# Mixture-of-experts kernel on one core: the row gather for a later expert moved inside the branch on a pair's second expert, and the row transposes for a missing second expert put under a branch

## The chip, the cores and the metric

One Trainium2 chip, one of its cores. The metric is the device time of one execution of the whole program in microseconds (us), lower being better. Engines: TensorE (PE; its weight loads appear as PEld), VectorE (DVE), ScalarE (ACT), GpSimd (POOL) and SyncE (SP, which here issues most DMA transfers). A name that ends in q, as in POOLq or PEldq, is an engine's instruction sequencer: branches, register loads and semaphore instructions run there.

## The reference

The program is two stacks of layers over 256 latent tokens of 1024 elements; layer 0 of the first stack also carries 256 context tokens. Two layers of attention with a mixture of experts come first, then two layers of another mixer with a dense feed-forward part. The change is inside the mixture of experts, of which this is the core (512 tokens in layer 0, 256 in layer 1):

```python
e_in = jnp.take_along_axis(e_logits, g_idx[:, :, None], 1)[:, 0]
top_v, top_i = lax.top_k(e_in, TOP_K_IN_GROUP)          # 2 of the 8 experts of the chosen group
experts = g_idx * EXPERTS_PER_GROUP + top_i             # 32 experts in all
...
def expert_block(a):
    xb, e = a
    return (jax.nn.silu(xb @ w1[e]) * (xb @ w3[e])) @ w2[e]
...
return jnp.zeros((t, d), h.dtype).at[tok_s].add(w_s[:, None].astype(h.dtype) * yb[dest])
```

Each token goes through two experts; an expert that no token chose needs no work. The weights are 1024x512 (w1, w3) and 512x1024 (w2) in float32, 6 MB per expert.

## The kernel before, in words

The routing part of a layer puts the experts into an order of "slots" and leaves the number of rows of each slot in a small table (`meta2`; `meta` for slots 0 and 1). The number of used slots depends on the data, so the part that runs the experts is control flow: every engine loads the counts into registers (`load`, recorded at line L1096, an instruction TENSOR_LOAD) and branches.

Slots 0 and 1 run first (L1197 to L1199, before the change). The rest runs in pairs: `pair(k)` takes the even slot k and then the odd slot k+1, the latter only where its count is positive (L1188), and at its end (L1193, L1194) calls itself inside a branch for slot k+2, where that has rows. The program text therefore holds all pairs one inside the other, and the branch at L1194 that isn't taken leaves the whole of it.

A slot's work, `turn`, reads the slot's rows, already transposed, from a buffer `XT` (there are two, by the parity of the slot), multiplies by the expert's weights, which SP fetches in six pieces of 1 MB (`expert_weights`, issued at L143), and ends with a `scatter` on POOL (L1002), an indirect DMA that puts the result rows into the DRAM buffer `ybuf`. A turn has variants by the number of rows: `quarter1` and `quarter2` up to 32 rows (PE lines L1020, L1029, L1037), `half1` and `half2` up to 64 (L1048, L1056, L1063), `full1` and `full2` for 128 (L1073, L1081, L1088).

Rows come two slots ahead. `ahead(k)` makes POOL issue an indirect DMA (`gather`, L722) of the rows of slot k+2 into a buffer `XG` by parity, and `next_rows(k)` transposes the rows of slot k+1 from `XG` into `XT`: eight PE transposes (L997) and two ACT copies (L999). Inside a turn `next_rows` is called between the two halves of the matmuls. Where the second slot of a pair is missing, the `Else` of L1188 calls it alone, so that the pair's two ways leave the same buffers filled.

POOL, in a branch that doesn't issue the DMA which the other way of that branch issues, executes an instruction INC_SWDGE_SEM for it (ISA in the order of instructions). An unconditional branch closes each way.

After the last pair, `combine` (L1203) loads the result rows from `ybuf` into tiles `y` by SP (L1211); ACT scales one half (L1219), DVE adds the other and the residual (L1220 to L1222), a normalisation follows (POOL L213, ACT L345), and PE starts again with transposes of the normalised tile (L225).

Of the kernel before, what the change touches and what calls it, by code (L numbers as in the profile page):

```python
# [26 lines left out]
NE = 32  # L27
# [70 lines left out]
class Builder:  # L98
# [885 lines left out]
    def experts(self, l, nt, mp, first, meta, meta2, gtab, stabs, XG, XE, ybuf):  # L984
        tc, nc = self.tc, self.nc
        T = nt * P
# [3 lines left out]
        def gather(c, xg, rows=P):  # L990
            self.gather(self.fbuf, gtab, c, xg, rows)

        def rows_T(xg, xT, rows=P):
            for i in range(2):
                xb = self.bankB()[:, 0:4 * rows].rearrange("p (k t) -> p k t", k=4)
                for k in range(4):
                    nc.tensor.transpose(xb[:, k], xg[0:rows, (4 * i + k) * P:(4 * i + k + 1) * P],  # L997
                                        self.ident[0:rows, 0:rows])
                nc.scalar.activation(xT[:, 4 * i:4 * i + 4, 0:rows], xb, AF.Copy)  # L999
# [6 lines left out]

        def w2slice(W, k, a, n):
            return W[4 + k // 2][:, k % 2 * D + a:k % 2 * D + a + n]

        def wslice(W, m, k, a=0, n=512):  # L1010
            return W[2 * m + k // 4][:, k % 4 * 512 + a:k % 4 * 512 + a + n]

        def quarter1(W, xT, hT, between):

            acc = self.bankA()[:, 0:256]
            for k in range(KT):
                for m in range(2):
                    for f in range(2):
                        r = 64 * m + 32 * f
                        nc.tensor.matmul(acc[r:r + 32], lhsT=xT[:, k, 0:32], rhs=wslice(W, m, k, 256 * f, 256),  # L1020
                                         start=k == 0, stop=k == KT - 1)
            s = mp.tile([P, 512], F32, tag="s", name="s", bufs=1)[0:64, 0:256]
            nc.scalar.activation(s, acc[0:64], AF.Silu)  # L1023
            nc.vector.tensor_tensor(s, s, acc[64:128], ALU.mult)  # L1024
            between()
            hb = self.bankB()[:, 0:128].rearrange("p (k t) -> p k t", k=2)
            hT = hT[:, 0:2, 0:64]
            for i in range(2):
                nc.tensor.transpose(hb[:, i], s[:, i * P:i * P + P], self.ident[0:64, 0:64])  # L1029
            nc.vector.tensor_copy(hT, hb)  # L1030
# [64 lines left out]
        def load(src, i, hi, **k):  # L1095
            return nc.values_load(src[0:1, i:i + 1], min_val=0, max_val=hi,  # L1096
                                  skip_runtime_bounds_check_because=MADE, **k)
# [11 lines left out]
        def ahead(k):  # L1109
            if k + AHEAD < NE:  # L1110
                gather((k + AHEAD) * nt, XG[k % AHEAD], 64 if sized(k + AHEAD) == "small" else P)

        def next_rows(k):
            if k + 1 < NE:
                rows_T(XG[(k + 1) % AHEAD], XT[(k + 1) % 2], 64 if sized(k + 1) == "small" else P)
# [66 lines left out]
        def pair(k):  # L1182

            ahead(k)
            turn(k, sized(k), load(meta2, NE + k, T), self.expert_weights(wm, load(meta2, k, NE - 1, engines=[ENG.SP])))
            ahead(k + 1)
            n = load(meta2, NE + k + 1, T)
            with tc.If(n > 0) as some:  # L1188
                W = self.expert_weights(wm, load(meta2, k + 1, NE - 1, engines=[ENG.SP]))
                turn(k + 1, "small", n, W)  # L1190
            with some.Else():
                next_rows(k + 1)
            if k + 2 < NE:  # L1193
                with tc.If(load(meta2, NE + k + 2, T) > 0):  # L1194
                    pair(k + 2)
# [4 lines left out]
        with tc.If(load(meta2, NE + 2, T) > 0):  # L1200
            pair(2)
# [557 lines left out]
```

## Time and profile before

| | us |
|---|---|
| median of 3 runs | 2283.38 |
| lowest and highest of them | 2280.43, 2285.77 |
| the profiled execution, its own time | 2275.24 |
| its span, first to last instruction | 2272.8 |
| PE busy in the span | 1916.9 (84%) |
| DVE busy | 1006.2 (44%) |
| ACT busy | 732.1 (32%) |
| POOL busy | 263.4 (12%) |

The mean granted clock of TensorE was 0.923. The experts of layer 0 run from about 410 to 772 us, those of layer 1 from about 1040 to 1288 us. All times in this document are us from the start of the span, unless they are durations.

A line of a timeline reads: start, duration from the first to the last instruction of the group, engine, line, operation, output from input, count, and in brackets the idle time before it with what ended it. "issue" means that nothing the profile shows was waited for. A line of a view of one source line reads: line, engine, operation, count, shortest, median and longest duration in ns, and the first and last start in us.

### The profile page before, as it was taken

The page shows a single profiled execution, that of the slowest core. Times are in us where ns is not written, and L with a number is a line of the kernel's source. Part 1 is how long each engine was busy: PE and PEld are TensorE (multiplying, and loading weights), DVE is VectorE, ACT ScalarE, POOL GpSimd, SP SyncE. Part 2 cuts the span into 40 slices and gives each one's busy share as a digit, 9 for nine tenths or more (in the row PEclk, how much of TensorE's full clock was granted, in tenths as well). Part 3 has the DMA queues.
Part 4 walks back from the last instruction along what each step waited for, and adds up shares of the span by engine and source line. Part 5 has one row for each costly group of instructions (what it writes and reads, how often), then busy time and mean ns, then how long its engine had stood idle before and what let it go on. Part 6 is the DMA issues. An engine that isn't in the chain of part 4 may idle for free. (4 is left out here: it accounts for less than half of the span.)

```text
span 2272.8 us, 27150 instructions
## 1 busy us (share of the span) xinstructions
PE 1916.9 (84%) x10066; PEld 1338.3 (59%) x10066; DVE 1006.2 (44%) x1968; ACT 732.1 (32%) x1304; POOL 263.4 (12%) x205
## 2 busy tenths in 40 slices
PE   6999797778886489967766479998999799998997
PEld 2656475433443177753333267786788677776886
DVE  3346655310000275661000257656554566566554
ACT  2233432100111254411101255444444454444442
POOL 0002401001101152120111102001000020002000
PEclk9999798799998799977988889999999999998999
DMA  9973214454779651156689754254455344444550
GB/s 395 378 294 127 105 38 180 174 197 186 310 283 402 254 219 44 40 222 266 263 326 411 286 191 146 96 196 170 167 186 184 129 163 145 134 164 166 185 178 26
DMA packets 74302, 456.06 MB, mean 201 GB/s; under 512 B 12696, under 2 KB 13244, under 8 KB 23648
## 3 DMA queue, kind: packets, MB, share of 16 engines
q1 hardware_dynamic: 61632, 430.99, 50.5%
q0 software_dynamic: 8816, 14.79, 1.8%
q10 hardware_dynamic: 3632, 7.37, 0.9%
q8 instruction: 133, 2.18, 0.4%
q14 instruction: 89, 0.73, 0.1%
HBM read 452.77 MB, written 13.30 MB: 205 GB/s over the span
## 5 line engine op out<-in xcount | busy, mean ns | idle before, releaser
L167 DVE TENSOR_TENSOR whl<-w,whl 128x1024 fp32r<-128x1024 f32 x312 | 396.4, 1284 | 230.1 <-ACT whl L166 220.3
L166 ACT ACTIVATE whl<-w 128x1024 fp32r<-128x1024 f32 x332 | 344.5, 1057 | 262.5 <-PE bankA L180 206.7
L178 PE MATMUL bankA<-whl,x2h 128*128 128x512 f32 (+1 forms) x864 | 344.3, 399 | 9.6 <-ACT x2h L238 7.2
L180 PE MATMUL bankA<-whl,x2l 128*128 128x512 f32 (+1 forms) x864 | 343.6, 398 | 5.8 <-DVE x2l L239 5.8
L179 PE MATMUL bankA<-whl,x2h 128*128 128x512 f32 (+1 forms) x864 | 341.1, 396 | 0.0
L178 PEld LDWEIGHTS bankA<-whl,x2h 128*128 128x128 f32 x864 | 167.8, 194 | 43.5 <-ACT x2h L238 8.2
L180 PEld LDWEIGHTS bankA<-whl,x2l 128*128 128x128 f32 x864 | 166.8, 193 | 40.4 <-DVE x2l L239 7.2
L1073 PE MATMUL bankA<-w,xt 128*128 128x512 f32 x320 | 155.3, 647 | 39.3 <-issue 31.5
L179 PEld LDWEIGHTS bankA<-whl,x2h 128*128 128x128 f32 x864 | 167.2, 194 | 34.3 <-issue 2.0
L1073 PEld LDWEIGHTS bankA<-w,xt 128*128 128x128 f32 x320 | 65.7, 208 | 126.4 <-issue 125.4
L178 PE MATMUL bankA<-whl,xh 128*128 128x512 f32 (+1 forms) x336 | 131.7, 392 | 5.1 <-ACT xh L238 5.1
L1020 PE MATMUL bankA<-w,xt 128*32 128x256 f32 x1216 | 88.4, 445 | 54.7 <-issue 47.2
L179 PE MATMUL bankA<-whl,xh 128*128 128x512 f32 (+1 forms) x336 | 128.7, 383 | 5.1 <-DVE whl L167 5.1
L180 PE MATMUL bankA<-whl,xl 128*128 128x512 f32 (+1 forms) x336 | 127.6, 384 | 0.0
L414 ACT ACTIVATE p<-bankS,sm 128x256 f32<-128x256 f32 (+2 forms) x160 | 85.6, 536 | 116.9 <-DVE sm L405 60.1
L213 POOL TENSOR_TENSOR sm<-sm,mhalf 128x1 f32<-128x1 f32 (+3 forms) x32 | 32.1, 1003 | 686.7 <-DVE sm L211 675.0
L1020 PEld LDWEIGHTS bankA<-w,xt 128*32 128x32 f32 x1216 | 48.9, 127 | 94.4 <-issue 74.6
L1077 DVE TENSOR_TENSOR s<-s,bankA 128x512 f32<-128x512 f32 x10 | 6.9, 688 | 200.6 <-PE bankA L1073 188.0
L1002 POOL DMA_INDIRECT ybuf<-ys,stab x34 | 34.8, 1023 | 499.7 <-ACT xt L999 124.8
L1024 DVE TENSOR_TENSOR s<-s,bankA 64x256 f32<-64x256 f32 x19 | 8.0, 423 | 177.0 <-ACT s L1023 177.0
L178 PEld LDWEIGHTS bankA<-whl,xh 128*128 128x128 f32 x336 | 63.8, 190 | 31.8 <-ACT xh L238 7.1
L1088 PE MATMUL bankA<-w,ht 128*128 128x512 f32 x160 | 71.3, 599 | 7.8 <-DVE ht L1082 7.8
(462 smaller groups left out, 2907.3 us busy)
## 6 DMA issues: line engine op xcount, KB each, us to landing
w<-in_wmoe SPq DMA_DIRECT2D x174, 1024.0 KB, 14.9
w<-in_wd SPq DMA_DIRECT2D x166, 1024.0 KB, 5.5
w<-in_wmod SPq DMA_DIRECT2D x48, 1024.0 KB, 9.1
y<-ybuf SPq DMA_DIRECT2D x12, 512.0 KB, 10.6
w<-in_rows SPq DMA_DIRECT2D x5, 1024.0 KB, 5.3
w<-mrow SPq DMA_DIRECT2D x7, 512.0 KB, 8.5
fbuf<-w SPq DMA_DIRECT2D x4, 512.0 KB, 2.9
nb<-in_nabias POOLq DMA_DIRECT2D x16, 128.0 KB, 2.4
```

Of the source, the lines that this page charges most:

```text
L166: nc.scalar.activation(h, s, AF.Copy)
L167: self.low = (eng or nc.vector).tensor_tensor(lo, s, h, ALU.subtract).ins
L178: mm(out, lhsT=xh, rhs=wh, start=start, stop=False)
L179: mm(out, lhsT=xh, rhs=wl, start=False, stop=False)
L180: mm(out, lhsT=xl, rhs=wh, start=False, stop=stop)
L213: self.power = self.nc.gpsimd.tensor_tensor(r, t, self.mhalf[:, :n], ALU.pow).ins
L414: nc.scalar.activation(p[:, :n], s[i][:, :n], AF.Exp, bias=nm[:, i:i + 1], accum_out=ss[:, i:i + 1])
L1002: nc.gpsimd.indirect_dma_start(out=ybuf.rearrange("r (m d) -> (r m) d", m=1 << parts), out_offset=bass.IndirectOffsetOnAxis(ap=stabs[parts ...
L1020: nc.tensor.matmul(acc[r:r + 32], lhsT=xT[:, k, 0:32], rhs=wslice(W, m, k, 256 * f, 256), start=k == 0, stop=k == KT - 1)
L1024: nc.vector.tensor_tensor(s, s, acc[64:128], ALU.mult)
L1073: nc.tensor.matmul(acc[m], lhsT=xT[:, k], rhs=wslice(W, m, k), start=k == 0, stop=k == KT - 1)
L1088: nc.tensor.matmul(yb[m], lhsT=hT[:, k], rhs=w2slice(W, k, m * 512, 512), start=k == 0, stop=k == 3)
```

## The change

`ahead(k + 1)`, the gather of the rows of slot k+3, moves from ahead of the branch on the second slot into its taken side. On the other side, the same gather and the transposes `next_rows(k + 1)` stand under a further branch, on whether slot k+2 has rows.

```diff
             ahead(k)
             turn(k, sized(k), load(meta2, NE + k, T), ...)
-            ahead(k + 1)
             n = load(meta2, NE + k + 1, T)
             with tc.If(n > 0) as some:
+                ahead(k + 1)
                 W = self.expert_weights(wm, load(meta2, k + 1, NE - 1, engines=[ENG.SP]))
                 turn(k + 1, "small", n, W)
             with some.Else():
-                next_rows(k + 1)
+                if k + 2 < NE:
+                    with tc.If(load(meta2, NE + k + 2, T) > 0):
+                        ahead(k + 1)
+                        next_rows(k + 1)
             if k + 2 < NE:
                 with tc.If(load(meta2, NE + k + 2, T) > 0):
                     pair(k + 2)
```

After the change, the branch on the second slot is recorded at L1187 (L1188 before), the new branch at L1193, and the branch to the next pair at L1197 (L1194 before).

On POOL, between the end of a pair's first turn and the second turn, where `meta` is the table of counts, `xg` a gather's destination and `fbuf` the rows in DRAM, this stood before:

```order
L1163 UNCONDITIONAL_BRANCH
L722 DMA xg_0_3069<-fbuf_315,gtab_3293 64x1024
L1096 TENSOR_LOAD meta_3295
L1188 COMPARE_AND_BRANCH
L1167 COMPARE_AND_BRANCH
```

and this stands now:

```order
L1163 UNCONDITIONAL_BRANCH
L1096 TENSOR_LOAD meta_3295
L1187 COMPARE_AND_BRANCH
L722 DMA xg_0_3069<-fbuf_315,gtab_3293 64x1024
L1167 COMPARE_AND_BRANCH
```

The gather went from ahead of the load and the branch to behind both.

On POOL, from the last scatter of the second turn through the side for a missing second slot to the branch to the next pair, before:

```order
L1002 DMA ybuf_3064<-ys,stab_3363 4096x256
L1167 UNCONDITIONAL_BRANCH
L1188 ISA
L1188 UNCONDITIONAL_BRANCH
L1096 TENSOR_LOAD meta_3295
L1194 COMPARE_AND_BRANCH
```

and now:

```order
L1002 DMA ybuf_3064<-ys,stab_3363 4096x256
L1167 UNCONDITIONAL_BRANCH
L1096 TENSOR_LOAD meta_3295
L1193 COMPARE_AND_BRANCH
L722 DMA xg_0_3069<-fbuf_315,gtab_3293 64x1024
L1187 ISA
L1193 UNCONDITIONAL_BRANCH
L1193 ISA
L1187 ISA
L1193 UNCONDITIONAL_BRANCH
L1096 TENSOR_LOAD meta_3295
L1197 COMPARE_AND_BRANCH
```

The side for a missing slot had one ISA; it now has a load, a branch, and behind it either the gather and one ISA or two ISA.

On PE, at the same place, where `cst` holds the identity matrix of the transposes, before and now in one piece:

```order
 L1167 UNCONDITIONAL_BRANCH
+L1096 TENSOR_LOAD meta_3295
+L1193 COMPARE_AND_BRANCH
 L997 MATMUL bankB<-cst,xg_0_3068 128x128 x8
-L1188 UNCONDITIONAL_BRANCH
+L1193 UNCONDITIONAL_BRANCH x2
 L1096 TENSOR_LOAD meta_3295
-L1194 COMPARE_AND_BRANCH
+L1197 COMPARE_AND_BRANCH
```

The eight transposes now stand behind a load and a branch. The same two rows and one more closing branch come on every engine in every pair of the program text (28 pairs in two layers); the order of the other instructions on each engine is as before.

## Rows read from the trace of the kernel before

**Rows 1.** The page: busy time and share of the span, by engine.

```profile
PE 1916.9 (84%) x10066; PEld 1338.3 (59%) x10066; DVE 1006.2 (44%) x1968; ACT 732.1 (32%) x1304; POOL 263.4 (12%) x205
```

**Rows 2.** One source line, the branch on the second slot (L1188), whole span.

```profile
L1188 PEldq COMPARE_BRANCH  x13: 65/75/4361, 550.6 to 1266.7; - x13
...
L1188 POOLq COMPARE_BRANCH  x13: 34/34/45, 553.5 to 1267.9; - x13
...
L1188 POOLq INC_SWDGE_SEM  x1: 1320/1320/1320, 765.9 to 765.9; - x1
```

**Rows 3.** Timeline of PE, 755 to 800 us.

```profile
767.28 1.94 PE L997 MATMUL bankB<-cst,xg 128*128 128x128 f32 x8 [5.28 <-issue]
789.32 1.97 PE L225 MATMUL bankB<-cst,hlat 128*128 128x128 f32 x8 [20.09 <-ACT hlat L345]
```

**Rows 4.** Timeline of all engines, 755 to 800 us.

```profile
763.00 1.00 POOL L1002 DMA_INDIRECT ybuf<-ys,stab  x1 [10.71 <-POOLq L1177]
765.55 0.97 POOL L722 DMA_INDIRECT xg<-fbuf,gtab  x1 [1.55 <-issue]
...
769.32 0.60 ACT L999 ACTIVATE xt<-bankB 128x512 f32<-128x512 f32 x1 [0.23 <-PE bankB L997]
772.90 1.39 SPq L1211 DMA_DIRECT2D y<-ybuf  x2
...
776.56 1.15 ACT L1219 ACTIVATE y<-y,rw 128x1024 f32<-128x1024 f32 x1 [6.64 <-DMA y<-ybuf]
...
779.93 1.29 DVE L1220 SCALAR_TENSOR_TENSOR y<-y,rw 128x1024 f32<-128x1024 f32 x1 [21.64 <-DMA y<-ybuf]
```

**Rows 5.** The branch to the next pair (L1194), 740 to 800 us: sequencers.

```profile
L1194 POOLq EVENT_SEMAPHORE  x5: 17/42/43, 770.8 to 771.1; - x5
...
L1194 PEldq COMPARE_BRANCH  x3: 65/203/4062, 746.1 to 772.1; - x3
...
L1194 PEldq EVENT_SEMAPHORE  x2: 51/51/51, 771.8 to 772.0; - x2
...
L1194 POOLq INC_SWDGE_SEM  x1: 1348/1348/1348, 771.2 to 771.2; - x1
```

**Rows 6.** The gather's line (L722), 740 to 800 us: the register move ahead of each.

```profile
L722 POOLq MOVE  x2: 29/29/29, 750.3 to 764.7; - x2
```

**Rows 7.** The loads of counts (L1096) on POOL, 740 to 800 us.

```profile
L1096 POOLq TENSOR_LOAD <-meta x4: 287/292/298, 749.9 to 767.2; - x4
```

**Rows 8.** Timeline of all engines at the exit from layer 1's experts, 1276 to 1312 us.

```profile
1281.75 0.99 POOL L1002 DMA_INDIRECT ybuf<-ys,stab  x1 [12.50 <-ACT ys L1066]
...
1288.52 0.82 SPq L1211 DMA_DIRECT2D y<-ybuf  x2
```

**Rows 9.** L1194 at that exit, 1260 to 1300 us.

```profile
L1194 POOLq INC_SWDGE_SEM  x1: 2317/2317/2317, 1285.9 to 1285.9; - x1
```

**Rows 10.** Timeline of POOL, 1235 to 1300 us: a gather between the turns of a pair.

```profile
1244.44 0.97 POOL L722 DMA_INDIRECT xg<-fbuf,gtab  x1 [0.30 <-issue]
```

**Rows 11.** The gather's line (L722), 1240 to 1260 us: from issue to landing.

```profile
DMA to landing us min/median/max: 8.5/8.6/8.7
```

**Rows 12.** Timeline of PE, 1241 to 1282 us: the transposes of those rows.

```profile
1262.51 0.71 PE L997 MATMUL bankB<-cst,xg 64*128 64x64 f32 x8
```

**Rows 13.** PE's branch between a turn's variants (L1177), 660 to 757 us.

```profile
L1177 PEldq COMPARE_BRANCH  x3: 68/77/82, 689.0 to 746.7; - x3
```

**Rows 14.** The same branch, 1040 to 1160 us.

```profile
L1177 PEldq COMPARE_BRANCH  x3: 439/4183/6785, 1051.9 to 1127.1; - x3
```

**Rows 15.** Timeline of PE, 686 to 757 us: first matmuls of two turns.

```profile
689.77 3.66 PE L1020 MATMUL bankA<-w,xt 128*32 128x256 f32 x64 [0.55 <-ACT ys L1040]
...
702.86 6.49 PE L1020 MATMUL bankA<-w,xt 128*32 128x256 f32 x64 [5.70 <-issue]
```

**Rows 16.** A window; the last columns are granted clock, DMA share, GB/s.

```profile
690.00:757.00 67.00, 48.34 (x418) 21.82 (x410) 3.63 (x9) 8.05 (x19) 10.07 (x10) 0.85 0.96 386
```

## The prediction

> **What bounds the kernel now.** I began with the busy shares: PE works 84% of the span and POOL 12% [rows 1], so a saving on POOL or in the transposes counts only where PE stands waiting for it. The next question was how often the changed code runs, and the line of the branch on the second slot answers it: it was met 13 times, and the instruction that stands in for a scatter not issued, which only the side for a missing slot has, ran once, at 765.9 us [rows 2]. Of 13 pairs, 12 have both slots. What the change can remove is thus one gather, eight transposes and two copies, at one place: the exit from layer 0's experts.
>
> That exit is read from the timelines. PE's last transposes start at 767.28 and take 1.94 us; then PE stands idle 20.09 us, until the normalised tile gives it work at 789.32 [rows 3]. What PE waits for is a chain: the last scatter starts at 763.00, SP issues the loads of the result at 772.90, ACT takes the first at 776.56, DVE the second at 779.93 [rows 4]. The 9.90 us from scatter to load are the stretch on which the change acts. The sequencers say what fills them. POOL issues the gather (its register move at 764.7, its DMA at 765.55 [rows 4, 6]), loads a count (0.29 us [rows 7]), branches, spends 1.32 us on INC_SWDGE_SEM [rows 2], takes the far branch out of all pairs, handles semaphores from 770.8, and spends another 1.348 us on an INC_SWDGE_SEM from 771.2, so until 772.5 [rows 5]. PE's branch at L1188 took 4.361 us and its branch at L1194 4.062 us; its closing semaphores came at 771.8 to 772.0 [rows 2, 5]. So POOL ends last, PE 0.5 us ahead of it, and the load follows POOL by 0.4 us. The transposes and copies are followed by idle PE and ACT (the copy at 769.32 is over 3 us before the load is issued, and ACT then waits for the load [rows 4]).
>
> **The change part by part.**
>
> *Taken pairs (12).* The gather goes behind a count's load of 0.29 us and a near branch of 0.034 us [rows 2, 7], some 0.4 us with the gaps. A gather at 1244.44 lands 8.6 us later, at about 1253.0, and its rows are transposed at 1262.51 [rows 10 to 12]: 9.5 us to spare. What stands behind the gather on POOL is that turn's scatter, some 12 us later. Cost: 0. One more closing branch per engine and pair is below 0.1 us and is covered by the same slack, or by the stream of weights.
>
> *POOL at the exit, removed.* From the register move at 764.7 to the branch at 765.7 is 1.0 us, of which the load and the branch are 0.29 and 0.045, which stay. The gather's dispatch is the rest: **-0.65 us**. Its transfer has no reader.
>
> *POOL at the exit, added.* The side for a missing slot now has a load and a branch, 0.3 + 0.05 us, and about 0.15 us between them: **+0.5 us**. And it has two ISA where there was one, a stand-in for the gather beside that for the scatter: **+1.32 us** by the one at this place [rows 2]. The bounds of the second are 0 (were two back to back to go as one) and 2.32 us, the longest of its kind [rows 9]; I take 1.32 as the nearest. The new branch skips a few instructions, as near ones do that took 0.034 us; were it like PE's far ones, it would be 4.1 us, the upper bound.
>
> The sum on POOL is -0.65 + 0.5 + 1.32 = +1.2 us: it ends at 773.7 instead of 772.5.
>
> *PE at the exit.* The eight transposes go; a load of 0.3 us and a branch come. The branch jumps over eight transposes and their weight loads, a short way: 0.075 us is the median of such short ones [rows 2]. The far branch of 4.06 us stays. PE would end at about 772.4 instead of 772.0, ahead of POOL's 773.7, so it adds nothing. At 4.1 us for the new branch it would end at 776.4, which is +3.9 on the load.
>
> *Downstream.* The loads, ACT, DVE and PE's restart follow in one chain; nothing in the 20.09 us gives room, so the +1.2 us passes on whole.
>
> *Everything else: the place of code.* The added rows lie in all 28 pairs of the program text, and PE's later code moves. That could matter, since PE's branches cost very unequal amounts: at L1177 the same source line took 0.068 to 0.082 us between 660 and 757 us, and up to 6.785 us between 1040 and 1160 us [rows 13, 14]. PE waits then for nothing that the profile shows (5.70 us of "issue" ahead of a turn [rows 15]). Which of these stalls come and go can't be read from the rows. [...]
>
> I put the net at 0, with bounds of one stall gained or lost: -6.8 to +6.1 us. Much of it is covered besides: from 690 to 757 us the DMA engines are 96% busy at 386 GB/s [rows 16], so a turn that stalls there finds its weights ready afterwards and catches up, and one that stalls less waits for weights.
>
> **Sum.** +1.2 us. On the profiled execution, 2275.2 + 1.2 = 2276.4. That execution is 8.1 us (0.36%) faster than the median of the runs, 2283.4, and below all three; so I put the term on the median: **2284.6 us**. A measurement of this kernel can tell about 0.2%, 4.6 us, from no change; the forecast is no measurable change.
>
> **Rivals.**
>
> *No stand-in on the path (faster, but within 0.2%).* At layer 1's exit, where the second slot exists, scatter to load takes 1288.52 - 1281.75 = 6.77 us [rows 8] against 9.90 in layer 0. If the removed gather and transposes are what makes the difference, the exit gains 3.1 us: 2280.3. Against it: on POOL the gather is 0.65 us, and the idle of 5.28 us on PE [rows 3] is the branch's 4.36, which stays.
>
> *A stall less (faster).* The code of layer 1 moves by more rows than that of layer 0, as the additions pile up. If the 6.785 us branch at 1127.08 [rows 14] becomes a near one ahead of which PE was not waiting for weights, the time is 2284.6 - 6.8 = 2277.8. For it: the stretch up to 1160 us is not full of transfers, so nothing else holds PE there. Against it: the moved code may fall no better, and the stream of weights that follows may take part of it back.
>
> *A stall more (slower).* The turn that starts at 689.77 waits 0.55 us, for ACT, behind a branch of at most 0.082 us [rows 13, 15]; the turn at 702.86 waits 5.70 us with nothing to wait for. If moved code makes the first like the second, PE loses up to 6.1 us: 2284.6 + 6.1 = 2290.7. It decides from the point at which the stall outlasts what the weights behind it would have made PE wait anyway; at 96% DMA share from 690 us [rows 16] that cover is large, which speaks against. The new branch on PE at the exit, dear at 4.1 us, is a smaller form of it: 2283.4 + 3.9 = 2287.3.
>
> *The change does nothing.* With 12 of 13 pairs taken, the removed work exists once. That is the forecast's ground, and would give 2283.4; it is within the forecast.
>
> **How the numbers follow.** The forecast, an exit between 0 and +2.2 us and stalls that cancel or hide, has 0.60; the shorter exit (2280.3) 0.05; a dear branch at the exit alone (2287.3) 0.04: these three are within 0.2%, 0.69 less a little for their edges, so 0.66. A stall less (2277.8) has 0.17, a stall more (2290.7) 0.17. The range, 2277 to 2291, takes in both and leaves out combinations of two stalls and measurement scatter at the ends, less than 2 in 10.
>
> **What would show it.** Right: no gather and no L997 between 763 and 790 us; on POOL two INC_SWDGE_SEM of some 1.3 us one behind the other where there was one; the load of the result at 10.5 to 11.5 us behind the last scatter instead of 9.90; gathers of taken pairs some 0.4 us later, with no wait of PE behind them. Wrong: a distance from scatter to load near 7 us, or above 13 us; PE's L1193 branch in microseconds; a change in PE's idle "issue" ahead of turns between 410 and 760 or 1040 and 1276 us whose sum reaches the starts of the exits, by more than 2 us.

## The result and the profile after

| | before | after |
|---|---|---|
| median, us | 2283.86 (6 runs) | 2304.52 (6 runs) |
| lowest and highest | 2280.43, 2285.77 | 2297.05, 2308.26 |
| profiled span | 2272.8 | 2305.1 |
| mean granted TensorE clock | 0.923 | 0.910 |

The ratio is 1.0088, with a 95% interval of 1.0073 to 1.0103: the change makes the kernel about 20 us slower, where 2284.6 with at most 2291 was forecast. All medians of before in the sections below lie between 2282.0 and 2282.7; I take 2282.5 for it.

The page after, to be read against [rows 1]: PE does 8 matmuls fewer (10058 for 10066), POOL one gather fewer (204 instructions for 205), and the span is longer all the same.

```profile
span 2305.1 us, 27211 instructions
...
PE 1927.0 (84%) x10058; PEld 1344.1 (58%) x10058; DVE 1004.8 (44%) x1968; ACT 730.8 (32%) x1302; POOL 262.1 (11%) x204
```

First the place on which the prediction's sum was made, the exit from layer 0's experts. The timeline of all engines after, which answers to [rows 4]:

```profile
776.04 1.00 POOL L1002 DMA_INDIRECT ybuf<-ys,stab  x1 [10.71 <-POOLq L1177]
...
786.57 0.81 SPq L1214 DMA_DIRECT2D y<-ybuf  x2
```

and the lines of the new branch (L1193) and of the branch on the second slot (L1187), 760 to 800 us, which answer to [rows 2]:

```profile
L1193 POOLq INC_SWDGE_SEM  x1: 1300/1300/1300, 778.8 to 778.8; - x1
L1193 PEldq COMPARE_BRANCH  x1: 231/231/231, 779.8 to 779.8; - x1
```
```profile
L1187 PEldq COMPARE_BRANCH  x1: 2822/2822/2822, 776.6 to 776.6; - x1
...
L1187 POOLq INC_SWDGE_SEM  x1: 1295/1295/1295, 780.1 to 780.1; - x1
```

Two INC_SWDGE_SEM of 1.3 us stand one behind the other where there was one, the gather and the transposes are gone, and the load comes 10.53 us behind the scatter instead of 9.90: +0.6 us. On POOL the stretch from the scatter's start to the end of these stand-ins took 5.4 us for 4.2 [rows 2, 4], which is the forecast's +1.2; the stretch from there to POOL's next semaphores took 3.1 us for 3.6 [rows 5]:

```profile
L1197 POOLq EVENT_SEMAPHORE  x5: 17/42/43, 784.5 to 784.8; - x5
```

But the scatter itself starts at 776.04 instead of 763.00. Thirteen microseconds were lost ahead of the place of the change, 2.9 of them ahead of layer 0's experts.

PE's timeline from 645 to 765 us shows where; it answers to [rows 15]:

```profile
690.54 1.93 PE L1037 MATMUL bankA<-w,ht 128*32 128x256 f32 x32 [0.39 <-DVE ht L1030]
698.93 5.43 PE L1020 MATMUL bankA<-w,xt 128*32 128x256 f32 x64 [6.46 <-DMA w<-in_wmoe]
...
714.99 4.49 PE L1020 MATMUL bankA<-w,xt 128*32 128x256 f32 x38 [6.90 <-issue]
...
732.20 5.86 PE L1020 MATMUL bankA<-w,xt 128*32 128x256 f32 x64 [6.20 <-DMA w<-in_wmoe]
...
747.44 8.52 PE L1048 MATMUL bankA<-w,xt 128*64 128x512 f32 x32 [5.66 <-issue]
```

The turn that waited 0.55 us at 689.77 in the kernel before [rows 15] now waits 6.46. The profile names a DMA, but PE's sequencer was held until 0.3 us before the turn began: the line of the branch ahead of that turn (L1167, a window of 1.5 us around it), before and after:

```profile
L1167 PEldq COMPARE_BRANCH  x1: 227/227/227, 689.1 to 689.1; - x1
```
```profile
L1167 PEldq COMPARE_BRANCH  x1: 6127/6127/6127, 692.5 to 692.5; - x1
```

The same happens at the next such place (before 0.227 us at 712.9, after 5.877 at 726.1) and in layer 1, for instance at L1177:

```profile
L1177 PEldq COMPARE_BRANCH  x1: 439/439/439, 1082.9 to 1082.9; - x1
```
```profile
L1177 PEldq COMPARE_BRANCH  x1: 6690/6690/6690, 1103.2 to 1103.2; - x1
```

These are branches that the change doesn't touch, with the same outcome in both kernels. What goes with a long one can be seen among the transfers. In the window of the near L1167 branch (before, 688.6 to 690 us) the view of DMA queues has no packet of a queue of the kind "instruction"; in that of the long one (after, 692.5 to 698.7 us) it has, among others:

```profile
q8 instruction: 1, 0.02, 1.1%
```

This is a packet of 16,384 bytes that starts 3.75 us into the branch and takes 1.1 us. In the fourteen traces of this document 285 of PE's branches took over 1.5 us; in 281 of them, among these all 20 of before and all 23 of after, a packet of this queue and size starts and ends inside the branch, 1.2 to 1.9 us before its end, and in the other four one that had started up to 0.7 us ahead of the branch ends inside it. So a long branch goes with such a packet; that PE waits for it isn't shown.

Added up over the trace, PE's branches of over 0.9 us (the "long" ones from here on) come to 101.6 us before (22 of them) and 123.8 after (24): 22.2 us more, about what the kernel lost. Matched one by one, four near branches became long (at 689.1, 712.9, 1082.9 and 1233.0 us before) and two long ones near (1116.8 and 1219.1); the six long ones up to 612 us kept their lengths, 24.3 us in sum before and 24.5 after. By stretches, from PE's first work for an expert to PE's restart behind the exit: layer 0 took 789.32 - 424.62 = 364.70 before and 802.62 - 427.54 = 375.08 after, layer 1 took 1305.85 - 1031.10 = 274.75 and 1336.46 - 1047.34 = 289.12. That is 24.8 of the 32.3 us between the two profiled spans. The other 7.5 us lie in stretches with the same instructions in both kernels. In the profile of the same changed kernel in another run (e8 below, a span of 2292.9 us) they come to 0.7 us, and the two stretches to 19.4, so most of the 7.5 is scatter between executions.

### The profile page after: what moved, and what is told of

Same layout as the page of the kernel before. It is cut to its first block, busy times and chain, and to the rows that moved or that the text cites. A ratio compares the mean times of both kernels' runs of the same rounds, so it can differ in the third digit from the quotient of the medians.

```text
span 2305.1 us, 27211 instructions
## 1 busy us (share of the span) xinstructions
PE 1927.0 (84%) x10058; PEld 1344.1 (58%) x10058; DVE 1004.8 (44%) x1968; ACT 730.8 (32%) x1302; POOL 262.1 (11%) x204
## 5 line engine op out<-in xcount | busy, mean ns | idle before, releaser
L167 DVE TENSOR_TENSOR whl<-w,whl 128x1024 fp32r<-128x1024 f32 x312 | 395.0, 1280 | 233.1 <-ACT whl L166 223.7
```

Source lines behind the costliest of these rows:

```text
L167: self.low = (eng or nc.vector).tensor_tensor(lo, s, h, ALU.subtract).ins
```

## The experiments

**Theory A.** The change lengthens PE's program in each of its 28 pairs, and all code behind moves; of PE's 231 branches in the two traces 185 took 0.07 to 0.44 us and 43 took 2.7 to 7.4, and if that goes by where the code lies, more of them are long now. **Theory B** (the rival): the gather that comes later, or POOL's added branches and stand-ins, costs the 20 us.

### The two halves of the change

The gather's half (e1) leaves PE's program as it was:

```diff
-            ahead(k + 1)
             n = load(meta2, NE + k + 1, T)
             with tc.If(n > 0) as some:
+                ahead(k + 1)
...
             with some.Else():
+                ahead(k + 1)
                 next_rows(k + 1)
```

> The gather moved into both sides of the branch, the transposes for a missing second slot unconditional: PE's program has the same instructions at the same places as the kernel before (16830 in both), POOL's has the moved gather. Theory A (PE's program got longer, its code lies elsewhere, and branches that were near now stall): 2284 +-4 us, PE's stalling branches where they were before. Theory B (the later gather, or POOL's branches, cost the 20 us): 2300 or more.

The branch's half (e2) leaves the gather where it was:

```diff
             with some.Else():
-                next_rows(k + 1)
+                if k + 2 < NE:
+                    with tc.If(load(meta2, NE + k + 2, T) > 0):
+                        next_rows(k + 1)
```

> The gather stays ahead of the branch, only the transposes for a missing slot go under the new branch: PE's program is that of the change (17066 instructions), POOL's gathers stand as before. Theory A: 2300 to 2308 us, with PE's stalls where the change has them. Theory B: 2284 +-4 us.

Measured: e1 2281.54 us, ratio 0.9996 (0.9983 to 1.0009), so nothing; e2 2296.85 us, ratio 1.0076 (1.0055 to 1.0098). The lines of the two branches shown above, L1177 in e1 and L1167 and L1177 in e2:

```profile
L1177 PEldq COMPARE_BRANCH  x1: 442/442/442, 1085.6 to 1085.6; - x1
```
```profile
L1167 PEldq COMPARE_BRANCH  x1: 7036/7036/7036, 693.4 to 693.4; - x1
```
```profile
L1177 PEldq COMPARE_BRANCH  x1: 6112/6112/6112, 1099.7 to 1099.7; - x1
```

With PE's old program the branch is near (0.44 us), with its new one it is dear (6.11), whatever POOL's gather does. Theory B falls as the cause of most of the loss, as far as the gather goes; POOL's added branch is in e2 as well, and what rules it out is e4 below, which has all of POOL's program of the change. e2 missed its expectation from below, by 3 us.

### Moving code without changing what runs

If place alone decides, then instructions that are never executed must do it too. I put them into the third continuation of slot 0 of layer 0, which these counts never reach, as tiny transposes of two instructions each (`range(64)` for 128):

```diff
+                if l == 0 and k == 0 and g == 3:
+                    pads = [self.bankB() for _ in range(3)]
+                    for j in range(64):
+                        nc.tensor.transpose(pads[j % 3][0:32, 0:32], self.ident[0:32, 0:32], self.ident[0:32, 0:32])
```

In the kernel before, 128 of them:

> The kernel before with 128 more PE instructions (64 transposes with their weight loads) in the third continuation of slot 0 of layer 0, a place that is never executed. Nothing that runs is changed. Theory A: the time differs from 2284 by more than 5 us either way, and PE's long branches (over 1 us) are others than before from 470 us on. Theory B, or a cost of what is executed: 2284 +-4 us.

In the changed kernel, 128:

> The changed kernel with the same 128 PE instructions that are never executed. Theory A: the time differs from 2304 by more than 5 us, most likely down, since the changed kernel's positions are among the dear ones. Theory B: 2304 +-5 us.

Measured: e3 2266.53 us, ratio 0.9937 (0.9912 to 0.9962); e4 2283.28 us, ratio 1.0008 (0.9996 to 1.0020). Dead code made the kernel before 16 us faster and the changed one 21 us faster; with it the change, POOL's program and all, takes the time of the kernel before. One of the branches that changed, before and in e3 (where the pad's lines shift L1177 to L1181):

```profile
L1177 PEldq COMPARE_BRANCH  x1: 6758/6758/6758, 465.4 to 465.4; - x1
```
```profile
L1181 PEldq COMPARE_BRANCH  x1: 411/411/411, 469.3 to 469.3; - x1
```

and PE's first matmuls behind it, on its timeline, before and in e3:

```profile
472.84 7.65 PE L1073 MATMUL bankA<-w,xt 128*128 128x512 f32 x13 [8.30 <-issue]
```
```profile
470.26 10.11 PE L1073 MATMUL bankA<-w,xt 128*128 128x512 f32 x23 [1.89 <-DVE hctx L350]
```

The idle time named "issue" was the branch: 8.30 us with it, 1.89 without, and in that place a wait of another engine's tile.

Then 256, to see whether the long branches come back, and 192 and 64:

> The kernel before with 256 PE instructions that are never executed, at the same place as the 128. [...] Theory A2 (the amount of code matters, the more dead code the faster or the slower): not 2282; by the trend of the 128, near 2251 us.

> 192 PE instructions that are never executed. Theory A: another set of long branches, a time that differs from 2282 us by the difference of the sums of PE's branches over 0.9 us (101.6 us in the kernel before, 85.7 with 128), within 4 us. A rival that long branches and time have little to do with one another: time and that sum differ by more than 8 us.

> 64 PE instructions that are never executed. As with 192: theory A: a time of 2282 us plus the change in the sum of PE's branches over 0.9 us against the 101.6 us of the kernel before, within 4 us.

Measured: e5 2280.29 us, ratio 0.9984 (0.9969 to 0.9998); e6 2277.11 us, ratio 0.9989 (0.9974 to 1.0004); e7 2280.93 us, ratio 0.9993 (0.9980 to 1.0006). With 256 the kernel comes back to within 2.4 us of its time, and nearly all of its long branches come back too. L1167 in the kernel before and the same line (L1171) in e5, over the whole span:

```profile
L1167 PEldq COMPARE_BRANCH  x40: 65/228/6537, 550.7 to 1277.2; - x40
```
```profile
L1171 PEldq COMPARE_BRANCH  x40: 65/234/6313, 553.3 to 1282.9; - x40
```

The sums of the long branches are 101.6 and 101.4 us. The time alone wouldn't show a return, since 64 and, below, 96 instructions give 2280.9 and 2280.1 us too; the branches do. Matched one by one with those of the kernel before, one of 115 changes sides of 0.9 us with 256 (0.44 us becomes 1.26), and 15 to 21 do with 64, 96, 128, 160 and 192. So it is the place of the code that counts, and not its amount, by whose trend 2251 us was expected; a shift by 256 gives back the long branches, shifts by 64 to 192 don't. No other multiple of 256 was run, and what in a place makes a branch long isn't shown.

### The remaining 8 us, and more places

The change once more beside these, and then the change without the gather on the side for a missing slot (`ahead(k + 1)` under the new branch taken out):

> The changed kernel once more, on the chip of these runs. The run with the new branch alone (PE's program the same as the change's) gave 2296.9 us, the change itself 2304.5 in another set of runs. If the gather's part adds nothing and the rest is scatter: 2295 to 2302 us here. If POOL's program with its further branch costs some 6 us: 2302 to 2308 us.

> The change without the gather on the side for a missing second slot (with these counts that gather is never issued; it is left out of the program, and with it the second INC_SWDGE_SEM). PE's program is that of the change, and the gather of taken pairs stands behind the branch as in the change; POOL's program is shorter by two rows per pair. The run with the new branch alone gave 2296.9 us, the change 2304.5 and 2305.5. If the 8 us between them are POOL's added code: 2295 to 2299 us. If they are the gather's place in taken pairs (which alone gave no difference in e1): 2302 to 2308 us, with PE's L1177 branch near 1150 us at 4 us or more as in the change, where the branch alone had 0.46.

Measured: e8 2305.49 us (2294.76 to 2308.86), ratio 1.0106 (1.0083 to 1.0128); e9 2299.23 us (2289.67 to 2304.86), ratio 1.0069 (1.0039 to 1.0099). The executions of these three kernels (e2, e8, e9) scatter by 7 to 15 us and overlap; e9 lies between the two answers. At one place the traces differ: PE's L1177 near 1150 us takes 0.464 us in e2's and 4.422 and 4.622 in those of e8 and e9, though PE's program is the same in all three. In e2 a packet of the queue "instruction" had moved at 1146.37 us, 2 us ahead of the branch; in e8 and e9 it moves inside the branch (1149.98 and 1155.73). So the place of code isn't all that decides. The traces of before and after also have 19 records BRANCH_PREFETCH_HINT each on PE; no run set out to remove them, and what part they have isn't shown. That one branch could be 4 of the 8 us, and it goes with the gather's place in taken pairs, as it does in e9; but one profiled execution each doesn't settle it.

The granted clock has a part in this too. The three executions of the change in which it was 0.918 or 0.919 took 2294.8 to 2297.9 us, against 2294.3 for the one of e2 at 0.918; the other eight, at 0.910 to 0.915, took 2303.0 to 2308.9. At like clocks little of the 8 us is left. Thirteen executions of the kernel before at 0.918 or 0.919 have a median of 2283.4, so some 14 us of the change's loss are there at the same clock, and the rest goes with a lower one; whether the longer waits lower it isn't shown, and in e9 the times don't follow the clock. This part stays open.

Two more pads of the kernel before and one of the changed kernel:

> The kernel before with 96 PE instructions that are never executed. Theory A: 2282.5 us plus the sum of PE's branches over 0.9 us less 101.6 us, within 4 us; by its neighbours (64: 2280.9, 128: 2266.5) between them.

> 160 PE instructions that are never executed. Theory A: the same relation between sum of long branches and time, within 4 us; by its neighbours (128: 2266.5, 192: 2277.1) between them.

> The changed kernel with 192 PE instructions that are never executed. Theory A: 2282.5 us plus the sum of PE's branches over 0.9 us less 101.6 us, within 4 us; with 128 it was 2283.3, with none 2305.

Measured: e10 2280.06 us, ratio 0.9992 (0.9974 to 1.0010); e11 2273.08 us, ratio 0.9961 (0.9939 to 0.9983); e12 2275.01 us, ratio 0.9957 (0.9939 to 0.9975).

### Long branches against time

The sum is over PE's branches of more than 0.9 us in each profiled execution; "by the sum" is 2282.5 + sum - 101.6.

| kernel | sum, us | by the sum | median | off |
|---|---|---|---|---|
| before | 101.6 | 2282.5 | 2282.5 | |
| the change | 123.8 | 2304.7 | 2304.5 | -0.2 |
| e8, the change again | 125.0 | 2305.9 | 2305.5 | -0.4 |
| e1, gather's half | 100.8 | 2281.7 | 2281.5 | -0.2 |
| e2, branch's half | 119.2 | 2300.1 | 2296.9 | -3.2 |
| e9, no gather for a missing slot | 123.5 | 2304.4 | 2299.2 | -5.2 |
| e3, before + 128 | 85.7 | 2266.6 | 2266.5 | -0.1 |
| e5, before + 256 | 101.4 | 2282.3 | 2280.3 | -2.0 |
| e6, before + 192 | 98.3 | 2279.2 | 2277.1 | -2.1 |
| e7, before + 64 | 98.0 | 2278.9 | 2280.9 | +2.0 |
| e10, before + 96 | 94.9 | 2275.8 | 2280.1 | +4.3 |
| e11, before + 160 | 95.7 | 2276.6 | 2273.1 | -3.5 |
| e4, change + 128 | 101.5 | 2282.4 | 2283.3 | +0.9 |
| e12, change + 192 | 80.9 | 2261.8 | 2275.0 | +13.2 |

Most lie within 4 us; e10 misses by 4.3, e9 by 5.2, and e12, the one with the smallest sum, by 13. The table is weaker than it looks. Each sum is of one execution and each time a median of several, which lie up to 15 us apart. The times of e6, e7 and e10 can't be told from the kernel before by their intervals. And by layers the relation is loose: in e3 layer 0's sum fell by 2.4 us and its stretch by 9.9, layer 1's by 13.5 and 4.2. The sum tells the size and the direction of a large shift, not the time of a kernel.

The view of PE's waits in layer 1 tells what became of e12's gain there, where the sum fell by 16.8 us and the stretch by 1.0. Before (1031 to 1283 us):

```profile
PE bankA L1020 <- issue: 37.5, 11, 6.4
PE bankA L1073 <- issue: 14.7, 3, 7.0
```

and in e12 (1031 to 1280 us; the columns are the total in us, the times, the longest):

```profile
PE bankA L1020 <- issue: 16.4, 5, 6.1
PE bankA L1020 <- DMA w<-in_wmoe: 13.6, 4, 5.7
PE bankA L1073 <- DMA w<-in_wmoe: 12.7, 2, 10.8
...
PE bankA L1073 <- issue: 1.9, 1, 1.9
```

"Issue" falls by 33.9 us on these two lines, and 26.3 us named as waits for weights stand in its place. The name misleads for 18.5 of them, as it did at 698.93: these three waits last until a long branch ends, or 1.1 us more at most. The other 7.9 us have no long branch ahead. The stretch from 1160 us on shows the limit better, in e12 and before (the last columns are granted clock, DMA share, GB/s):

```profile
1160.00:1270.00 110.00, 71.41 (x851) 36.76 (x842) 5.71 (x16) 13.08 (x32) 17.35 (x18) 0.84 1.01 407
```
```profile
1160.00:1276.00 116.00, 75.04 (x888) 41.95 (x888) 6.85 (x18) 14.28 (x35) 17.97 (x18) 0.85 0.98 393
```

The turn that starts at 1202.67 us in e12 is 21.4 us ahead of the same turn before (1224.06); the one at 1263.63 is only 3.4 ahead (1267.03). In between, with the DMA engines at a share of 1.01 and 407 GB/s, PE gave back most of what it had gained. So in e12 the gain of the shorter branches was largely lost again in layer 1, where PE's waits named for weights grew from 0.4 us to 26.3, 7.9 of them with no long branch ahead.

The kernel before with 128 dead PE instructions is the best that was run: 2266.53 us, faster than before by 0.6% and 38 us below the median of the change. The change with 192 is faster than before as well, by 0.4%.

## Why the prediction was wrong

*How often the changed code runs: right.* One gather and eight matmuls less, at one exit.

*The exit: right in its parts, a little large.* -0.65 and +0.5 on POOL could not be told apart from the rest, the second INC_SWDGE_SEM took 1.30 us as forecast 1.32, PE's new branch 0.231 us, at the near end of its range, not the far one of 4.1. The sum on POOL was +1.2 us, as forecast; the stretch behind it, which the prediction held fixed, was 0.5 us shorter, so that scatter to load grew by 0.6 us. PE's two long branches there became shorter, 2.82 and 3.45 us, for 4.36 and 4.06 [rows 2, 5], but PE was not last, nor was it forecast to be.

*Taken pairs: right.* The gather's half alone gave 0.9996. A closing branch is indeed below 0.1 us on POOL: behind the INC_SWDGE_SEM of L1188, which ends at 767.19 us before, the next load starts 0.04 us later, with the closing branch in between.

*"Everything else: the place of code ... I put the net at 0, with bounds of one stall gained or lost": the step that failed.* The kernel lost 20.7 us, of which the exit has 0.6, and the sum of PE's long branches grew by 22.2. I had the rows that show that the same branch costs 0.07 or 6.8 us [rows 13, 14], and I had the change put rows into all 28 pairs. From this it did not follow that one stall would come or go: four came and two went, and others grew or shrank. Rows 13 and 14 are of L1177 alone, too. In layer 0 it was L1167, the next branch, that became long; two of its long ones, of 6.07 and 6.02 us, already stood between 690 and 757 us in the kernel before, and no row shows them. PE's 22 long branches of 101.6 us were a stock, and the change shuffled a part of it, all of it from 689 us on; the size of that stock, not that of its largest member, was the scale for the bounds. The kernels of the table spread from -16 to +23 us around the kernel before.

*"Much of it is covered besides ... a turn that stalls there finds its weights ready afterwards and catches up": right about the weights, wrong about the catching up.* A DMA share of 0.96 [rows 16] says that the stream was busy, not that PE stood waiting for it. PE's waits in that window of the kernel before (690 to 757 us) have little of that; the "issue" lines hold the two long branches:

```profile
PE bankA L1048 <- issue: 6.9, 2, 5.4
PE bankA L1020 <- issue: 6.0, 2, 5.7
PE bankA L1020 <- DMA w<-in_wmoe: 2.4, 1, 2.4
```

In the changed kernel the stream ran on behind the stalled PE, in the same window at a share of 1.00 and 400 GB/s:

```profile
690.00:757.00 67.00, 38.33 (x392) 18.95 (x391) 2.79 (x8) 6.64 (x17) 8.02 (x8) 0.82 1.00 400
```

SP's timeline has its last issues of weights in layer 0, before and after:

```profile
601.41 139.20 SPq L143 DMA_DIRECT2D w<-in_wmoe  x48
```
```profile
692.53 51.11 SPq L143 DMA_DIRECT2D w<-in_wmoe  x20
```

They end at 740.6 and 743.6 us, 3.0 us apart, while the last scatters are 13.0 apart. Nor were the weights late behind the two new stalls: the turns at 698.93 and 732.20 begin 0.3 us behind the ends of their branches, though the profile names a DMA. PE was 3.3 us behind the kernel before at its turn of 685.20 us (681.95 before), 18.9 behind at that of 732.20 (713.31 before), and 13.0 at the scatter. So 5.9 of 15.6 us came back and 9.8 stayed. Weights that lie ready can only give back what PE would have waited for them, and that was little here. The other half of the forecast's sentence, that a turn "that stalls less waits for weights", is what e12 shows in layer 1.

*The rival "a stall more"* named the right place (the turn at 689.77) and the right price (6.1 us, which no row shows, but which fits the L1167 branch of 6.07 us at 695.7; the branch ahead of the turn took 6.13). It was one of several, and the cover that I held against it gave back only a part. The rival "a stall less" had the right cause and the wrong sign for layer 1; its stretch was indeed not full of transfers (a DMA share of 0.63 at 252 GB/s from 1040 to 1160 us before). It was also in reach: e3 is that case.

## What to carry to other kernels

In a kernel whose time goes through many branches, an edit that adds instructions to every unrolled block is an edit to the place of all code behind it. Add up PE's long branches over the trace before costing anything else: their total, not one of them, is the scale of what a shift can do (here -16 to +23 us of 101.6). Before crediting or blaming a change of a per cent in such a kernel, run the old kernel with dead instructions in a place that is never reached; here that alone moved it from 2282 to 2266 us, so one run of each of two versions doesn't compare them. And how far a stream of transfers covers a stall is read from the waits of the stalled engine (2.4 us here), not from the share of time in which the stream is busy (0.96).

## What the runs showed of the hardware that was not expected

A packet inside a long branch: 281 of 285 branches of PE of over 1.5 us hold a packet of 16,384 bytes of the DMA queue "instruction", which ends 1.2 to 1.9 us before the branch. The return at 256: 256 dead PE instructions gave back the long branches (101.4 us in sum for 101.6, all but one of 115 on the same side of 0.9 us) and, within 2.4 us, the time of the kernel without them, while 128 gave 85.7 us and 2266.5. And the size of the effect: between the worst and the best of three places of one and the same executed work (the change with 0 and with 192 dead instructions) lie 30 us, 1.3% of the time.
